# Moving the top-k of one token block out of the front of a decoder layer into its dense expert stage

## The chip, the cores and the metric

The kernel runs on one core of a Trainium2 chip. The metric is the device time of one execution in microseconds (us). The engines are named as in the profile: PE is TensorE (matmuls), DVE is VectorE, ACT is ScalarE, POOL is GpSimd, SP is SyncE (here only a queue that issues DMAs). Each engine works through its own list of instructions in order; an instruction that has to wait holds up all that stand behind it on its engine.

## What is computed

One layer of a hybrid decoder on 1024 tokens of width 1024, in float32. Its last part, where this change lies, is an expert layer (PEER) with 16384 experts of one neuron each:

```
def block(t):                                   # 128 tokens
    q = (t @ w_q).reshape(tb, 8, 2, 64)
    s = einsum('thcd,hckd->thck', q, keys)      # 8 heads, 2 halves, 128 keys
    top_s, top_i = top_k(s, 16)
    cand_s = top_s[:, :, 0, :, None] + top_s[:, :, 1, None, :]
    cand_i = top_i[:, :, 0, :, None] * 128 + top_i[:, :, 1, None, :]
    best_s, pos = top_k(cand_s, 16)
    idx = take_along_axis(cand_i, pos)          # 128 experts for each token
    g = softmax(best_s)
    act = gelu(einsum('thkd,td->thk', u_tab[idx], t))
    return einsum('thk,thkd->td', g * act, v_tab[idx])
```

Ahead of it stand a gated MLP and a state-space layer with their projections; behind it a gated residual and a final RMSNorm.

## The kernel before

The tokens are 8 blocks of 128. For blocks 0 to 4 the expert layer is computed **densely**: for each of 128 expert tiles (128 experts each) `stage1(i)` multiplies all 640 tokens by the tile's u (48 matmuls of 128x320 into `pa`, as three products of a high and a low part), applies the gelu, and `weigh` (L962) multiplies by the weights `Gt` (L968) and splits the result into `wh` and `wl` (L972). After every four tiles `stage2(g)` multiplies by their v rows (120 matmuls of 128x512 into `res` and `pd`). `load_u` and `load_v` load a tile's u and v, cast the high part on ACT (L925, L933) and subtract it on DVE (L926, L934); these are called the splits of u_i and v_i. For blocks 5, 6 and 7 the chosen rows are **gathered**: POOL issues indirect DMAs of two rows a step for each token (L878), DVE multiplies them by the token (L889, tiles `ru`), ACT sums (L884), and later DVE adds the weighted v rows (L906, tiles `rv`, one instruction a row, 128 for each block). Four row buffers of two rows each go round.

Before either, `route(b)` makes the top-k of a block: DVE's MAX8, FIND_INDEX8 and MATCH_REPLACE8 on 128 scores (L1368 to L1372), the same on the 50 candidates of a head, a softmax and look-ups of the indices (L1383 to L1430); its score tiles are `scr`, its results `gw` and `ix`. For a dense block `scatter(b)` then spreads the weights over all experts: `hot` (L675) and `a` (L680) on DVE, `b` (L688) on ACT, a matmul into `pgs` (L690), a copy to `GS` (L693) on ACT, and a store to `G_d` in DRAM, from which `load_g` reads `Gt` (L959). Block 4's scatter is the last.

The front of the program (everything up to the first dense tiles) is written out by a planner: each item of `plan` has a due time and a duration, and the items' steps are issued in the order of these. The items r0 to r7 are the routes, s0 to s4 the scatters, `ld` the first five stage 1 tiles (the lead). The scheduler of the tile framework then sets each engine's order. The main loop does one tile a turn and pulls steps of `side_work()` (L861) in between: the routes that the plan left out, three of their yields to a step, then the pool of the top-k is released, the row buffers take its place, and the gathers follow, 256 steps for each block. The two lines of the loop and of the side work that the change's numbers enter are

```
for b in range(NDB + cfg["early"], NB):          # L862, NDB = 5, NB = 8
pull(int((i + 1) * cfg["per"]) - int(i * cfg["per"]))   # L1127
```

At the end (`stage2(31)`, `finish`) DVE applies the gate, the residual and the norm (L836, L837, L845) and the rows are stored.

Of the kernel before, what the change touches and what calls it, by code (L numbers as in the profile page):

```python
# [38 lines left out]
QG = 4  # L39
GP = 2  # L40
FMAX = 3.0e38
CFG = dict(xo=[2, 3, 4, 0, 1], gt=3, ss=7, hs=2, b1=6, nw=6, raw=1, ngb=3, rows=4, lead=5, per=6.3, dv=[6, 9, 9, 2, 99], early=2,
           hp=600, eo=(2, 4), em={2: 'pppxx', 4: 'Xpp'}, seg=4, plan=dict(
    op0=(-238.2, 44.5), sb0=(-21, 248.8), m5=(-490.1, 3.4), r0=(234.1, 82.1), op1=(132.1, 27.3), op2=(292.7, 7.7),
    sb1=(310, 10.8), op3=(364.9, 36.8), r1=(301.9, 79), s0=(261.5, 137.5), sb2=(303.2, 61.7), zv=(372.6, 16.7),
    r2=(434.5, 89.3), s1=(746.9, 213.2), zu=(417.8, 124.5), sb3=(451.1, 27.3), r3=(536.2, 48.7),
    s2=(469.7, 305.5), gl=(553.5, 5.5), op4=(543.1, 6.2), op5=(577.6, 1.8), sb4=(663, 101), r4=(445.7, 88.9),
    s3=(833.5, 73.1), op6=(590.2, 7.7), sb5=(768.6, 1.7), op7=(897.9, 60.4), sb6=(809.8, 27.4), sb7=(892.4, 30.9),
    gt=(858.2, 122), rel=(739, 334), s4=(981.8, 131.5), r5=(916.4, 58.6), r6=(989.9, 124.6), ld=(776, 675.7),
    oa0=(-275.5, 62.3), oa1=(155.8, 9.5), oa2=(314.1, 7), oa3=(240.1, 5.1), oa4=(394.7, 40.1), oa5=(594, 15.7),  # L50
    oa6=(572.9, 5.5), oa7=(898.3, 28.1), z0=(-1650.9, 29.9), f1=(-1496.2, 24.1), z1=(-1253, 33.5),
    pa=(-1479.5, 58), pb=(-1364.9, 1.6), pc=(-1507.3, 44.1), cs=(-1171.2, 4.5), lu=(-1201.3, 17.4),
# [44 lines left out]
@with_exitstack  # L97
def tile_hybrid_layer(ctx: ExitStack, tc: tile.TileContext, a, out, cfg=CFG):
    nc = tc.nc
# [1383 lines left out]
```

## Time and profile before

| | us |
|---|---|
| median of 3 runs | 2657.12 (2654.34 to 2663.97) |
| the profiled execution | 2654.11 |
| its span in the profile | 2652.3 |
| PE, DVE, ACT busy | 2533.5, 2267.9, 1312.1 |
| first split of a u tile (u0) on DVE | 843.29 |
| first stage 1 tile behind the lead (pa5) on PE | 918.04 |
| last split of a u tile (u127) | 2596.07 |
| last matmul starts | 2636.74 |

Times in the trace count from the start of the span. A row of the order of time is start, duration, engine, line, operation, tiles out and in, how many alike in a row, and in brackets the idle time of the engine before it and what ended that. Buffer numbers are left out of the tiles' names there.

### The profile page before, as it was taken

How to read it: one execution, taken by the hardware profiler on the slowest of the kernel's cores; microseconds unless marked ns; L12 is line 12 of the kernel's file. 1: busy time of each engine (PE TensorE's matmuls, PEld its weight loads, DVE VectorE, ACT ScalarE, POOL GpSimd, SP SyncE). 2: the span in 40 equal slices, each digit the busy share in tenths (PEclk: the TensorE clock that was granted, in tenths of full speed). 3: DMA queues.
4: the chain of work that ended last, by engine and by line, in shares of the span. 5: the costliest groups of instructions: out<-in, count | busy, mean ns of one | idle time of the engine just before them, and what ended most of it. 6: DMA issues, size and time to landing. Idle time of an engine off the chain costs nothing.

```text
span 2652.3 us, 39046 instructions
## 1 busy us (share of the span) xinstructions
PE 2533.5 (96%) x14119; PEld 2163.7 (82%) x14119; DVE 2267.9 (86%) x4215; ACT 1312.1 (49%) x2315; POOL 1175.1 (44%) x842
## 2 busy tenths in 40 slices
PE   6999999999877999999999999999999999999997
PEld 3557676578666898889999989999999989999996
DVE  7894699869899888879989788889999888899898
ACT  2311246578968467773222577762223767732222
POOL 0001000000000177786667577766665767776660
PEclk9996999999988999999999999999999999999999
DMA  9546233444646689999999899999998999999993
GB/s 365 108 153 186 98 122 108 121 140 131 178 119 192 227 322 328 342 335 362 345 332 378 324 335 335 324 366 355 339 358 327 330 345 339 331 366 350 343 365 138
DMA packets 301761, 726.85 MB, mean 274 GB/s; under 512 B 42448, under 2 KB 133072, under 8 KB 301152
## 3 DMA queue, kind: packets, MB, share of 16 engines
q0 software_dynamic: 112832, 411.09, 42.4%
q1 hardware_dynamic: 165600, 254.48, 28.6%
q10 hardware_dynamic: 23136, 58.79, 6.2%
q8 instruction: 111, 1.82, 0.3%
q14 instruction: 82, 0.67, 0.1%
HBM read 660.70 MB, written 62.39 MB: 273 GB/s over the span
## 4 chain that ended last, share of the span: by engine, by line
PE 50%; DMA 2%; DVE 2%; issue 1%; POOL 0%; ACT 0%; DVEq 0%; POOLq 0%; ACTq 0%
PE pa L949 25%; PE res L987 13%; PE pd L996 12%; DMA ru<-in_peer_u_dram,ix 2%; DVE ru L889 1%; POOL ru L878 0%; DVE x L845 0%; DVE u L926 0%; DVE wl L972 0%; DVE x L837 0%; DVE w L968 0%; DVE v L934 0%; DVE pd L836 0%; ACT u L925 0%; ACT v L933 0%
## 5 line engine op out<-in xcount | busy, mean ns | idle before, releaser
L878 POOL DMA_INDIRECT ru<-in_peer_u_dram,ix x384 | 639.3, 1665 | 892.3 <-issue 742.3
L949 PE MATMUL pa<-Th,u 128*128 128x320 f32 x4096 | 909.5, 309 | 3.8 <-DVE u L926 2.9
L949 PEld LDWEIGHTS pa<-Th,u 128*128 128x128 f32 x4096 | 687.2, 188 | 7.0 <-DVE u L926 3.5
L878 POOL DMA_INDIRECT rv<-in_peer_v_dram,ix x384 | 515.5, 1343 | 267.8 <-DVE gacc L906 185.7
L949 PE MATMUL pa<-Tl,u 128*128 128x320 f32 x2048 | 632.7, 309 | 0.0
L889 DVE TENSOR_TENSOR ru<-ru,hn 128x2048 f32<-128x2048 f32 x192 | 438.5, 2288 | 113.7 <-DMA ru<-in_peer_u_dram,ix 111.2
L884 ACT ACTIVATE jk<-ru 128x1024 bf16<-128x1024 f32 x384 | 405.5, 1056 | 211.0 <-issue 155.3
L906 DVE SCALAR_TENSOR_TENSOR gacc<-rv,act,gacc 128x1024 f32<-128x1024 f32 x381 | 488.7, 1283 | 7.5 <-DMA rv<-in_peer_v_dram,ix 1.7
L996 PE MATMUL pd<-v,wh 128*128 128x512 f32 x1280 | 403.6, 391 | 3.4 <-ACT v L933 1.8
L987 PE MATMUL res<-v,wh 128*128 128x512 f32 x1280 | 401.1, 390 | 0.8 <-ACT wh L970 0.8
L949 PEld LDWEIGHTS pa<-Tl,u 128*128 128x128 f32 x2048 | 384.7, 188 | 1.7
L996 PEld LDWEIGHTS pd<-v,wh 128*128 128x128 f32 x1280 | 239.1, 188 | 53.2 <-ACT v L933 2.2
L987 PEld LDWEIGHTS res<-v,wh 128*128 128x128 f32 x1280 | 239.9, 188 | 50.0 <-ACT wh L970 1.1
L951 ACT ACTIVATE w<-pa 128x320 f32<-128x320 f32 x256 | 108.8, 431 | 330.8 <-PE pa L949 329.5
L688 ACT ACTIVATE b<-hot,gT 128x128 f32<-128x128 f16 x520 | 234.1, 545 | 60.7 <-PE pgs L690 35.1
L996 PE MATMUL pd<-v,wl 128*128 128x512 f32 x640 | 249.0, 390 | 1.8 <-DVE wl L972 1.8
L987 PE MATMUL res<-v,wl 128*128 128x512 f32 x640 | 248.4, 390 | 1.9 <-DVE wl L972 1.9
L690 PE MATMUL pgs<-a,b 128*128 128x128 f32 x1280 | 188.4, 299 | 48.1 <-DVE a L680 22.9
L925 ACT CAST u<-ur 128x1024 fp32r<-128x1024 f32 x128 | 133.5, 1043 | 201.5 <-DMA ur<-in_peer_ut_dram 98.1
L690 PEld LDWEIGHTS pgs<-a,b 128*128 128x128 f32 x1280 | 169.5, 206 | 70.5 <-ACT b L688 35.9
L926 DVE TENSOR_TENSOR u<-ur,u 128x1024 fp32r<-128x1024 f32 x128 | 156.4, 1222 | 30.8 <-ACT u L925 30.4
L933 ACT CAST v<-vr 128x1024 fp32r<-128x1024 f32 x128 | 133.6, 1044 | 98.9 <-DMA vr<-in_peer_v_dram 81.7
(349 smaller groups left out, 3041.0 us busy)
## 6 DMA issues: line engine op xcount, KB each, us to landing
vr<-in_peer_v_dram SPq DMA_DIRECT2D x128, 512.0 KB, 6.8
ur<-in_peer_ut_dram SPq DMA_DIRECT2D x128, 512.0 KB, 6.7
G_d<-GS SPq DMA_DIRECT2D x40, 1024.0 KB, 8.3
Gt<-G_d ACTq DMA_DIRECT2D x64, 640.0 KB, 8.0
wada<-in_w_ada_dram SPq DMA_DIRECT2D x17, 1024.0 KB, 13.7
wo<-in_w_out_dram SPq DMA_DIRECT2D x8, 1024.0 KB, 4.9
ru<-in_peer_u_dram,ix POOLq DMA_INDIRECT x384, 7.6
rv<-in_peer_v_dram,ix POOLq DMA_INDIRECT x384, 7.7
```

Source lines behind the costliest of these rows:

```text
L688: A.activation(b1[:, n], hot[:, :, o + n], AF.Copy, scale=gT[:, s1 + o + n:s1 + o + n + 1])
L690: T.matmul(pg[:, o // 4, (o % 4) * P:(o % 4 + 1) * P], b1[:, o % 2], a1[:, o % 4], start=True, stop=True)
L878: G.indirect_dma_start(out=row[:, e], out_offset=None, in_=a[src], in_offset=bass.IndirectOffsetOnAxis(ap=ix[:, s0 + e:s0 + e + 1], axis=0))
L884: A.activation(junk, row[:, e], AF.Copy, accum_out=act[:, s + e:s + e + 1])
L889: V.tensor_mul(row, row, bcast(hn, 1, GP))
L906: V.scalar_tensor_tensor(ac, row[:, e], w, ac, op0=ALU.mult, op1=ALU.add)
L925: A.copy(u[:, 0], ur)
L926: V.tensor_tensor(u[:, 1], ur, u[:, 0].bitcast(F32), op=ALU.subtract)
L933: A.copy(v[:, 0], vr)
L949: T.matmul(pa[:, :NN], l[:, k, :], r[:, k, ns], start=(k == 0 and m == 0), stop=(k == KD - 1 and m == 2))
L987: T.matmul(res[tb][n], l[:, ts], r[:, n * 512:(n + 1) * 512], start=(g == 0 and q == 0 and m == 0), stop=(g == NGR - 1 and q == QG - 1 and ...
L996: T.matmul(po, l[:, ts], r[:, n * 512:(n + 1) * 512], start=(q == 0 and m == 0), stop=(q == QG - 1 and m == 2))
```

## The change

Three numbers of the configuration. `early` goes from 2 to 1, so `side_work` does the routes of blocks 6 and 7 and not of 7 alone, 20 steps instead of 10 ahead of 768 gather steps. The item r6 leaves the plan. `per` goes from 6.3 to 6.6.

```
-... lead=5, per=6.3, dv=[6, 9, 9, 2, 99], early=2,
+... lead=5, per=6.6, dv=[6, 9, 9, 2, 99], early=1,
...
-    gt=(858.2, 122), rel=(739, 334), s4=(981.8, 131.5), r5=(916.4, 58.6), r6=(989.9, 124.6), ld=(776, 675.7),
+    gt=(858.2, 122), rel=(739, 334), s4=(981.8, 131.5), r5=(916.4, 58.6), ld=(776, 675.7),
```

What this does to the engines' orders is seen at three places. The first is DVE just ahead of the first u split, at the end of block 4's scatter (`hot4`, `a1_4`; names that end in 6 before the number are block 6's top-k). Before:

```order
L680 TENSOR_TENSOR a1_4_100_6863<-iot_1808,It4_5371 128x512
L1396 TENSOR_REDUCE sm6_6880<-g6_6877 128x8
L1416 TENSOR_TENSOR mk6_6890<-mk6_6890,dd6_6887 128x2048
L680 TENSOR_TENSOR a1_4_104_6895<-iot_1808,It4_5371 128x512
L1397 RECIPROCAL sm6_6880<-sm6_6880 128x8
L675 TENSOR_TENSOR hot4_120_6963<-iot8_1810,Jt4_5372 128x1024
L680 TENSOR_TENSOR a1_4_108_6907<-iot_1808,It4_5371 128x512
L1421 TENSOR_TENSOR mk6_6890<-mk6_6890 128x1024
L1398 TENSOR_TENSOR g6_6877<-g6_6877,sm6_6880 128x128
L680 TENSOR_TENSOR a1_4_112_6926<-iot_1808,It4_5371 128x512
L1421 TENSOR_TENSOR mk6_6890<-mk6_6890 128x512
L926 TENSOR_TENSOR u0_7023<-ur0_7021,u0_7023 128x1024
```

After:

```order
L827 TENSOR_TENSOR Tl_6567<-t32_4_6836,Th_6566 128x8x128
L675 TENSOR_TENSOR hot4_112_6764<-iot8_1810,Jt4_5372 128x1024
L680 TENSOR_TENSOR a1_4_108_6750<-iot_1808,It4_5371 128x512
L675 TENSOR_TENSOR hot4_120_6793<-iot8_1810,Jt4_5372 128x1024
L680 TENSOR_TENSOR a1_4_112_6767<-iot_1808,It4_5371 128x512
L680 TENSOR_TENSOR a1_4_116_6779<-iot_1808,It4_5371 128x512
L680 TENSOR_TENSOR a1_4_120_6796<-iot_1808,It4_5371 128x512
L926 TENSOR_TENSOR u0_6842<-ur0_6840,u0_6842 128x1024
L680 TENSOR_TENSOR a1_4_124_6808<-iot_1808,It4_5371 128x512
L1368 MAX m6_7132<-scr6_0_7134 128x8 x4
```

Block 6's instructions have left the stretch ahead of u0; its first one stands two behind u0 now.

The second is DVE in the lead, from the split of u2 to that of u3, with the two products of the weights of tiles 0 and 1 (`w0` by `Gt0_0` and `Gt0_1`). Before:

```order
L926 TENSOR_TENSOR u2_7138<-ur2_7136,u2_7138 128x1024
...
L968 TENSOR_TENSOR w0_7026<-w0_7026,Gt0_0_7309 128x2x320
L1421 TENSOR_TENSOR mk6_6890<-mk6_6890 128x1024
L1371 MAX m7_7313<-scr7_2_7337 128x8 x4
...
L926 TENSOR_TENSOR u3_7196<-ur3_7194,u3_7196 128x1024
```

After:

```order
L968 TENSOR_TENSOR w0_6845<-w0_6845,Gt0_0_7128 128x2x320
L1368 MAX m6_7132<-scr6_4_7178 128x8 x4
L1369 MAX_INDEX ixs6_7133<-m6_7132,scr6_4_7178 128x8
L926 TENSOR_TENSOR u2_6957<-ur2_6955,u2_6957 128x1024
L1369 MAX_INDEX ixs6_7133<-m6_7132,scr6_4_7178 128x8 x3
L1370 MATCH_REPLACE scr6_4_7178<-m6_7132,scr6_4_7178 128x128
L968 TENSOR_TENSOR w0_6845<-w0_6845,Gt0_1_7130 128x2x320
...
L926 TENSOR_TENSOR u3_7015<-ur3_7013,u3_7015 128x1024
```

The product with `Gt0_1` stood behind u3 before, and stands ahead of it now; the one with `Gt0_0` has moved ahead of u2.

The third is DVE from the split of u127 to that of v126 (`rv2_n` are gathered v rows n and n+1 of the last block). Before, no L906 follows u127:

```order
L906 SCALAR_TENSOR_TENSOR gacc2_19251<-rv2_126_21547,act2_16883,gacc2_19251 128x1024 x2
L926 TENSOR_TENSOR u127_21830<-ur127_21828,u127_21830 128x1024
L1025 TENSOR_TENSOR acc_6657<-acc_6657,fin2_21552 128x512
L1025 TENSOR_TENSOR acc_6657<-acc_6657,fin2_21552 128x1024 x2
L968 TENSOR_TENSOR w124_21579<-w124_21579,Gt31_1_21639 128x2x320
L836 TENSOR_TENSOR gacc2_19251<-gacc2_19251,fin2_21552 128x1024
L934 TENSOR_TENSOR v125_21841<-vr125_21839,v125_21841 128x1024
```

After:

```order
L926 TENSOR_TENSOR u127_21830<-ur127_21828,u127_21830 128x1024
L968 TENSOR_TENSOR w124_21579<-w124_21579,Gt31_0_21637 128x2x320
L906 SCALAR_TENSOR_TENSOR gacc2_18917<-rv2_114_20990,act2_16549,gacc2_18917 128x1024
L968 TENSOR_TENSOR w124_21579<-w124_21579,Gt31_1_21639 128x2x320
L906 SCALAR_TENSOR_TENSOR gacc2_18917<-rv2_114_20990,act2_16549,gacc2_18917 128x1024
L906 SCALAR_TENSOR_TENSOR gacc2_18917<-rv2_116_20995,act2_16549,gacc2_18917 128x1024
L972 TENSOR_TENSOR wl62_21837<-w124_21579,wh62_21835 128x1280
L934 TENSOR_TENSOR v125_21841<-vr125_21839,v125_21841 128x1024
L906 SCALAR_TENSOR_TENSOR gacc2_18917<-rv2_116_20995,act2_16549,gacc2_18917 128x1024
L906 SCALAR_TENSOR_TENSOR gacc2_18917<-rv2_118_21063,act2_16549,gacc2_18917 128x1024 x2
```

The last row pairs, from half of 114 to 126, stand behind u127 now, 14 instructions of L906 in all up to the split of v127.

## Rows read from the trace of the kernel before

**Rows 1.** The page: the span, and the busy time of PE and DVE.

```profile
span 2652.3 us, 39046 instructions
...
PE 2533.5 (96%) x14119; PEld 2163.7 (82%) x14119; DVE 2267.9 (86%) x4215; ACT 1312.1 (49%) x2315; POOL 1175.1 (44%) x842
```

**Rows 2.** Busy time of each engine in four stretches (columns in the first row).

```profile
core 0: us, PE busy (x) PEld busy (x) DVE busy (x) ACT busy (x) POOL busy (x), PEclk, DMA share, GB/s
...
758.20:843.30 85.10, 61.05 (x400) 55.64 (x399) 79.38 (x353) 71.97 (x159) 0.00 (x0) 0.84 0.59 174
...
901.30:905.60 4.30, 4.27 (x12) 3.37 (x13) 3.46 (x7) 1.63 (x2) 0.00 (x0) 0.61 0.40 130
...
902.00:2602.00 1700.00, 1693.52 (x9517) 1546.25 (x9516) 1475.64 (x1203) 840.50 (x1328) 1157.57 (x773) 1.00 0.93 340
2602.00:2652.00 50.00, 35.13 (x174) 30.07 (x173) 39.31 (x120) 13.16 (x30) 1.58 (x3) 0.88 0.33 116
```

**Rows 3.** What ACT waited for from 758 to 843 us.

```profile
ACT b L688 <- DVE hot L675: 6.2, 5, 2.6
ACT tq L728 <- PE pq L726: 2.7, 2, 2.1
ACT GS L693 <- PE pgs L690: 2.7, 1, 2.7
ACT Th L826 <- DMA t<-T_d: 0.8, 2, 0.5
```

**Rows 4.** DVE in order of time: u0, w0 by Gt0_1, v3, u7, u11.

```profile
843.29 1.23 DVE L926 TENSOR_TENSOR u<-ur,u 128x1024 fp32r<-128x1024 f32 x1 [0.24 <-ACT u L925]
...
871.50 0.80 DVE L968 TENSOR_TENSOR w<-w,Gt 128x640 f32<-128x640 f32 x1
...
901.31 1.22 DVE L934 TENSOR_TENSOR v<-vr,v 128x1024 fp32r<-128x1024 f32 x1 [0.88 <-ACT v L933]
...
917.28 1.23 DVE L926 TENSOR_TENSOR u<-ur,u 128x1024 fp32r<-128x1024 f32 x1 [5.02 <-ACT u L925]
...
975.27 1.22 DVE L926 TENSOR_TENSOR u<-ur,u 128x1024 fp32r<-128x1024 f32 x1
```

**Rows 5.** ACT in order of time: the last GS copies, the loads of Gt.

```profile
857.64 1.07 ACT L693 COPY GS<-pgs 128x512 f32<-128x512 f32 x2
...
865.11 1.35 ACTq L959 DMA_DIRECT2D Gt<-G_d  x2
```

**Rows 6.** PE in order of time: around 902 us, pa5, pa11.

```profile
901.33 0.50 PE L996 MATMUL pd<-v,wh 128*128 128x512 f32 x1 [1.80 <-ACT v L933]
...
903.73 0.63 PE L996 MATMUL pd<-v,wl 128*128 128x512 f32 x1
904.16 0.63 PE L987 MATMUL res<-v,wh 128*128 128x512 f32 x1
...
918.04 0.30 PE L949 MATMUL pa<-Th,u 128*128 128x320 f32 x1
...
987.35 0.46 PE L949 MATMUL pa<-Th,u 128*128 128x320 f32 x2
```

**Rows 7.** The tile Gt from 850 to 890 us: issue to landing.

```profile
DMA to landing us min/median/max: 4.0/5.6/7.5
```

**Rows 8.** DVE's groups from 918 to 2653 us: the sums of gathered v rows.

```profile
L906 DVE SCALAR_TENSOR_TENSOR gacc<-rv,act,gacc 128x1024 f32<-128x1024 f32 x381 | 488.7, 1283 | 7.5 <-DMA rv<-in_peer_v_dram,ix 1.7
```

**Rows 9.** DVE in order of time: u127, v127, the first use of res, the last product.

```profile
2596.07 1.22 DVE L926 TENSOR_TENSOR u<-ur,u 128x1024 fp32r<-128x1024 f32 x1
...
2614.43 1.22 DVE L934 TENSOR_TENSOR v<-vr,v 128x1024 fp32r<-128x1024 f32 x1
...
2623.57 0.70 DVE L836 TENSOR_TENSOR res<-res,fin 128x512 f32<-128x512 f32 x1 [5.05 <-PE res L987]
...
2647.45 1.41 DVE L845 SCALAR_TENSOR_TENSOR x<-x,rf,fin 128x512 f32<-128x512 f32 x2
```

**Rows 10.** PE in order of time: the last matmul.

```profile
2636.74 0.39 PE L996 MATMUL pd<-v,wl 128*128 128x512 f32 x1
```

More of the change, by code (lines that the diff above doesn't have):

```diff
@@ L41 @@
 FMAX = 3.0e38
-CFG = dict(xo=[2, 3, 4, 0, 1], gt=3, ss=7, hs=2, b1=6, nw=6, raw=1, ngb=3, rows=4, lead=5, per=6.3, dv=[6, 9, 9, 2, 99], early=2,
+CFG = dict(xo=[2, 3, 4, 0, 1], gt=3, ss=7, hs=2, b1=6, nw=6, raw=1, ngb=3, rows=4, lead=5, per=6.6, dv=[6, 9, 9, 2, 99], early=1,
            hp=600, eo=(2, 4), em={2: 'pppxx', 4: 'Xpp'}, seg=4, plan=dict(
```

## The prediction

> **What bounds the kernel now.** I read the page, then busy time by stretch, then the waits of the stretch that the change touches, then single engines in order of time. The page says PE: busy in 2533.5 of 2652.3 us, VectorE (DVE) in 2267.9 [rows 1]. The stretches tell more [rows 2]. Between 902 and 2602 us, the dense stage, PE is busy in 1693.5 of 1700 us: it is the bound there, and DVE has 224 us to spare. In the 85 us before the first dense tile PE is busy 61 us, DVE 79 and ACT 72: this stretch waits for DVE and ACT. In the last 50 us PE is busy 35. So the change can act on the time in three places: the front, the lead of the dense stage, and the tail; in the middle only if it makes DVE late for PE.
>
> **The front (term A).** Until 758.2 us the orders of DVE, ACT and PE are the same in both kernels. From there to u0 (843.29, [rows 4]) DVE's order loses what route(6) had there: its first-level searches in 128 scores, those in the 50 candidates, the look-ups. Counted instruction by instruction in the order and priced at the step from one start to the next, that is 29 us of the 81.6 us so counted; 52.5 stay. If DVE were the only bound, the front would be 29 us shorter. It is not: ACT's order keeps the 109 or so scatter products of L688 (one or two more fall ahead of u0, 0.9 us), the GS copies and the rest, 72.0 us busy of 85.1 [rows 2]. Its waits in 758 to 843 us [rows 3] are 6.2 us for DVE's hot (L675), 2.7 for pgs from PE, 2.7 for a projection (pq) that stays where it is, and 0.8 for T's load. The first goes, since hot now stands behind less DVE work; the second goes too, since PE was late there because DVE's a (L680) was. A = 6.2 + 2.7 - 0.9 = 8 us earlier. Bounds: 4 if half of these waits come back as others, 12 if the other waits shown go too; ACT's 72.0 us of work allow no more than 13.
>
> **The lead (term B).** Before, the split of v3 stands 58.0 us behind that of u0 (901.31 - 843.29, [rows 4]), for 54.1 us of DVE work; stage2(0) ends, and pa5 begins, 15.6 us after v3 is done (918.04, [rows 6]). After, 55.4 us of work stand ahead of v3's split. What matters more is the place of `w0 x Gt0_1` (L968): 14.9 us of work behind u0 instead of 24.5 (before, it ran at 871.50, 28.2 us behind u0, without a wait [rows 4]). Its operand comes by a chain: the last GS copy on ACT at 857.64, the store into G_d on SP, the load issued on ACT at 865.11 when that store is in [rows 5], landing 4.0 to 7.5 us later, median 5.6 [rows 7]. Relative to u0 the last GS copy moves up only from 14.4 to about 10 us, because ACT's order ahead of it hardly changes. So the load is issued at about +17, and lands at about +23, with DVE in order and waiting from +15. The cast of u2 is behind that issue on ACT, and ur2's load is behind the stores on SP: u2 comes late too, within the same wait. So 8 us of waiting, of which 3.9 (58.0 - 54.1) were there before in other places: v3 would end 65.2 us behind u0 instead of 59.2, +6.0. Six matmuls with wl1 move behind v3, since wl1 comes just ahead of it: 6 x 0.23 = 1.4 us. B = +7. Bounds: 3 with the fastest landing, 11 with the slowest and u2 behind it.
>
> **The dense stage (term C).** Route(6) and route(7) together stand in front of the first gather now. Before, the first row pair is issued at 913.28 and the first product (L889) runs after u7; after, the product stands behind u10. PE must not wait for u11, the split right behind the first five products. Before, u11 ran at 975.27 and pa11 at 987.4 [rows 4, 6]. Relative to u0, u11 had ended at 133.2; after there are 11.4 us more DVE work ahead of it (121.3 against 109.9), so 144.6; pa11 is due at 144.1 + 7 = 151. Six us stay: C = 0. From there on the order shows the same work between two u's in both kernels: 3 row pairs a tile in the u phases, 6 or 7 rows a tile in the v phases. 6.6 instead of 6.3 steps a tile does not make them denser, since the gathers run as far behind program order as the row buffers put them. Bounds: -4 and +8.
>
> **The tail (term D).** This is the largest term. Before, all 384 v rows are summed ahead of the split of u127 (2596.07). After, 370 are: 14 of L906 stand behind it, between the last splits. One takes 1.283 us [rows 8]; 14 are 18.0. DVE's work behind u127 is 47.5 us before, and 65.8 after. Before, DVE ended 52.8 us after u127's start, 5.05 of it a wait for PE's res at 2623.57 [rows 9]. After, v127's split ends 31.4 us behind u127 (19.5 before), PE has 66 matmuls behind it, 15.0 us, and ends at 46.4 (before 41.0, [rows 10]). From v127 on DVE has 34.4 us of work for PE's 15, so it never waits: it ends at 66, not 52.8. D = 18.0 - 5.05 = +13. Bounds: 9 if u127 itself comes 3 to 4 us earlier (a product w124, for which DVE waited, no longer stands ahead of it), 16 if DVE still finds 3 us to wait.
>
> **Sum.** -8 + 7 + 0 + 13 = +12 us on the profiled execution's own 2654.1 us: 2666. The median of the runs is 3.0 us above that execution, so **2669 us** for a median, 0.45% slower. A measurement of this kernel tells about 0.5% (13.3 us) from no change, so this is just inside "same".
>
> **Rivals.**
> *The front frees what DVE loses.* If ACT had room (its copies faster once DVE's port is quieter, or L688 products ahead of 758), A would come to about 20, and B would hold: 20 - 7 - 13 = 0 gain, 2657. From A over 20 it turns to a gain; with all 29, 2648. For it: DVE is busy 79 of 85 us. Against: 72 us of ACT work that no order shortens [rows 2].
>
> *Slower: the dense stage gets late at u11.* The margin is 6 us, worked out from waits of before. If the first five row pairs, all issued within the top-k's end, land late by 3 us each, u11 is 9 us late, and PE, which is the bound from there on, never gets it back: C = +9, 2678. It decides once u11 is over 6 us later than I say. For it: before, DVE waited 5.02 us for u7's cast just there [rows 4]. Against: PE lost only 6.5 us in the 1700 us of the stage before [rows 2].
>
> *Slower: the clock in the tail.* After a gap of 1.8 us at 899 to 901 us the granted clock went to 0.61 for 4.3 us, and matmuls came every 0.43 us where they came every 0.23 [rows 2, 6]: 1.2 GHz in place of 2.4. In the tail PE would wait about 5 us for v127. If the 66 matmuls behind it ran at the lower level throughout, they would take 30 us, PE would end at 61, and DVE's last 11.8 us after it (2637.1 to 2648.9, [rows 9, 10]) make 73: D = +20, 2676. If the clock is low as briefly as at 902, nothing changes, since DVE ends at 66 anyway. The Trainium skill's page "TensorE: Matmul & The Clock Gate", section "Why this matters for your kernels", warns of idle gaps between bursts of matmuls in the middle of a kernel, since the engine falls back to its lower clock; by that rule the time would be the 2676 of this rival. The rows agree on the fall and show it as short.
>
> *The change does nothing to the middle* is part of the forecast: `per` alone moves no DVE instruction that PE waits for.
>
> **How the numbers follow.** The forecast has 0.6: its own range is 2656 to 2680, and it lies on the "same" side in 0.37 and on the slower one in 0.23. The rival of the front 0.13 (faster 0.05, same 0.08), of u11 0.17 (slower 0.14), of the clock 0.10 (slower 0.09). Together: faster 0.05, same 0.49, slower 0.46. All lowest bounds together give 2653, all highest 2688; the ends of 2652 and 2684 leave out about 2 in 10.
>
> **What would show it.** Right: u0's split near 835 with ACT still busy nearly all of the 80 us before it; a DVE wait at L968 or for u2 some 15 us behind u0; pa5 at about 917, near where it was; no PE wait at u11; then the same 55 us a group; behind u127 14 L906 among the v splits, PE waiting about 5 us for v127, DVE never idle, and an end 66 us behind u127's start. Wrong: u0 before 825 (A), pa5 10 us off (B), PE waits for u11 (C), or a tail in which u127 is 10 us earlier relative to PE than before (D).

## The result and the profile after

The changed kernel takes 2673.87 us (median of 7 runs, 2671.43 to 2677.61) against 2656.73 us: 1.0063 times the kernel before, 95% interval 1.0049 to 1.0076, which is 17 us slower. The profiled execution took 2675.51 us, 21.4 more than that of before. 3.6 us of this difference lie ahead of the change, in the part of the order that both kernels share. That part ends just behind block 5's score search; its last MAX8 is the mark from which I count below. DVE in order of time before the change:

```profile
747.87 0.28 DVE L1368 MAX8 m<-scr 128x8 f32<-128x128 f32 x1
```

The page of the changed kernel, and its busy time by stretch (columns as in rows 2). The front is taken from 761.83 us on: that is the place in the order which the kernel before reaches at 758.20, 3.63 us earlier, as at the mark.

```profile
span 2673.5 us, 39095 instructions
...
PE 2547.6 (95%) x14119; PEld 2173.6 (81%) x14119; DVE 2267.4 (85%) x4215; ACT 1315.3 (49%) x2317; POOL 1171.8 (44%) x842
```

```profile
761.83:842.37 80.54, 65.25 (x412) 58.74 (x411) 52.27 (x141) 71.88 (x160) 0.00 (x0) 0.82 0.59 176
...
800.00:842.40 42.40, 30.92 (x150) 25.87 (x149) 23.93 (x34) 42.40 (x93) 0.00 (x0) 0.76 0.72 219
```

Ahead of u0, DVE is busy 52.3 us where it was 79.4 [rows 2], and yet the stretch is only 4.5 us shorter: ACT has the same work (72.0 us before, 71.9 now), and is busy in 42.40 of the last 42.40 us. Its longest wait from 761.83 us on (the others add up to 0.7 us):

```profile
ACT tq L728 <- PE pq L726: 8.0, 2, 5.2
```

The waits for hot (6.2 in [rows 3]) and for pgs (2.7) are gone but for 0.2 us; the one for the projection pq grew from 2.7 to 8.0. PE in order of time shows why: in either kernel it works through 112 matmuls of pq in one piece. Before, and then after:

```profile
768.86 12.67 PE L726 MATMUL pq<-tq,wq 128*128 128x128 f32 x112
```

```profile
773.94 12.67 PE L726 MATMUL pq<-tq,wq 128*128 128x128 f32 x112
```

They end 33.7 us behind the mark before and 35.1 after. What ACT saves ahead of that place it spends there, waiting for pq. From there to u0 it is 61.8 us before and 55.8 after: these 6.0 us, less the 1.4 by which pq came later, are all that the front gains.

DVE in order of time: the mark, u0, u1, a wait for block 6's scores, u2, w0 by Gt0_1, v3, u11.

```profile
751.50 0.28 DVE L1368 MAX8 m<-scr 128x8 f32<-128x128 f32 x1
...
842.37 1.23 DVE L926 TENSOR_TENSOR u<-ur,u 128x1024 fp32r<-128x1024 f32 x1 [0.52 <-ACT u L925]
...
851.06 1.21 DVE L926 TENSOR_TENSOR u<-ur,u 128x1024 fp32r<-128x1024 f32 x1
...
867.54 0.87 DVE L1368 MAX8 m<-scr 128x8 f32<-128x128 f32 x4 [7.71 <-DMA scr<-sc_d]
868.60 1.21 DVE L926 TENSOR_TENSOR u<-ur,u 128x1024 fp32r<-128x1024 f32 x1
870.77 0.81 DVE L968 TENSOR_TENSOR w<-w,Gt 128x640 f32<-128x640 f32 x1
...
911.12 1.21 DVE L934 TENSOR_TENSOR v<-vr,v 128x1024 fp32r<-128x1024 f32 x1
...
985.32 1.22 DVE L926 TENSOR_TENSOR u<-ur,u 128x1024 fp32r<-128x1024 f32 x1
```

DVE stood still for 7.7 us, not at Gt0_1 but for scores, and u2's split began 17.5 us after u1's. SP's queue shows what lay ahead of both loads, and ACT's order when ur2 was in:

```profile
851.62 2.16 SPq L696 DMA_DIRECT2D G_d<-GS  x2
853.87 3.61 SPq L923 DMA_DIRECT2D ur<-in_peer_ut_dram  x1
857.58 1.91 SPq L762 DMA_DIRECT2D scr<-sc_d  x2
```

```profile
856.88 1.61 ACTq L959 DMA_DIRECT2D Gt<-G_d  x2
...
865.92 1.04 ACT L925 CAST u<-ur 128x1024 fp32r<-128x1024 f32 x1 [6.95 <-DMA ur<-in_peer_ut_dram]
```

The two last stores, 1 MB each, then ur2, then the scores. ur2's load came 12 us after its issue began, and the DMA engines were busy all that time (share 1.01; columns as in rows 2):

```profile
853.80:866.00 12.20, 5.40 (x37) 5.14 (x36) 4.05 (x24) 0.52 (x2) 0.00 (x0) 0.89 1.01 316
```

The longest of PE's waits from 843 to 927 us, for u2's cast, follows from it:

```profile
PE pa L949 <- ACT u L925: 7.8, 1, 7.8
```

PE in order of time: pa5, pa11, pa125, the last matmuls.

```profile
926.52 0.30 PE L949 MATMUL pa<-Th,u 128*128 128x320 f32 x1
...
995.83 0.46 PE L949 MATMUL pa<-Th,u 128*128 128x320 f32 x2
...
2601.54 0.30 PE L949 MATMUL pa<-Th,u 128*128 128x320 f32 x1
...
2656.90 0.39 PE L996 MATMUL pd<-v,wl 128*128 128x512 f32 x1
2657.13 0.62 PE L996 MATMUL pd<-v,wh 128*128 128x512 f32 x2
2657.58 0.39 PE L996 MATMUL pd<-v,wl 128*128 128x512 f32 x1
```

PE's longest wait in the tail:

```profile
PE pd L996 <- DVE x L837: 3.9, 1, 3.9
```

PE in order of time behind this wait, and the granted clock there (0.68, the column behind POOL's): from 2651.9 to 2654.9 us a matmul comes every 0.43 us, where it is 0.23 at the end of the tail.

```profile
2650.63 0.73 PE L996 MATMUL pd<-v,wh 128*128 128x512 f32 x2 [3.88 <-DVE x L837]
...
2653.21 0.63 PE L996 MATMUL pd<-v,wl 128*128 128x512 f32 x1
2653.64 1.05 PE L996 MATMUL pd<-v,wh 128*128 128x512 f32 x2
```

```profile
2650.00:2655.00 5.00, 4.37 (x13) 3.44 (x14) 4.93 (x24) 2.02 (x6) 0.00 (x0) 0.68 0.00 0
```

The tail on DVE: u127, v127, the first wait behind them, the last product; the wait of 5.05 us for res [rows 9] is gone.

```profile
2606.47 1.22 DVE L926 TENSOR_TENSOR u<-ur,u 128x1024 fp32r<-128x1024 f32 x1
...
2637.02 1.22 DVE L934 TENSOR_TENSOR v<-vr,v 128x1024 fp32r<-128x1024 f32 x1
...
2644.97 1.30 DVE L836 TENSOR_TENSOR res<-res,fin 128x512 f32<-128x512 f32 x2 [0.19 <-PE res L987]
...
2668.73 1.42 DVE L845 SCALAR_TENSOR_TENSOR x<-x,rf,fin 128x512 f32<-128x512 f32 x2
```

**The time by stage.** Five marks cut an execution: the MAX8 above, the start of u0's split, pa5, pa125 (the first stage 1 tile behind the second-last stage 2; 2588.62 before, the row below), and the end of DVE's last instruction.

```profile
2588.62 0.30 PE L949 MATMUL pa<-Th,u 128*128 128x320 f32 x1
```

So before: 843.29 - 747.87 = 95.4 us, 74.7, 1670.6 and 60.2. The same subtractions for every profiled execution (names as in the experiments below):

| | front | lead | dense stage | tail |
|---|---|---|---|---|
| before | 95.4 | 74.7 | 1670.6 | 60.2 |
| before, 14 rows cut | 95.0 | 74.3 | 1673.1 | 59.9 |
| before, b shared | 101.0 | 75.0 | 1672.5 | 59.9 |
| after | 90.9 | 84.1 | 1675.0 | 68.6 |
| after, pace 6.3 | 90.7 | 84.3 | 1675.4 | 68.6 |
| after, 14 rows cut | 91.9 | 84.1 | 1680.3 | 60.3 |
| after, stores by POOL | 91.5 | 80.5 | 1672.0 | 71.5 |
| after, ur by POOL | 91.9 | 81.2 | 1671.0 | 68.6 |
| after, b shared | 87.3 | 77.9 | 1672.8 | 67.9 |
| after, b shared, stores by POOL | 87.4 | 76.4 | 1670.4 | 69.0 |
| after, b shared, ur by POOL | 87.4 | 78.6 | 1672.5 | 67.9 |
| after, tail on POOL | 91.5 | 86.1 | 1682.5 | 74.0 |
| after, all three | 87.2 | 76.3 | 1668.7 | 74.1 |

Front, lead and tail repeat within about 2 us where the order is the same; the dense stage varies by several. The stretch ahead of the first mark (747 to 756 us) varies too. So the single stages say more than the totals.

### The profile page after: what moved, and what is told of

It reads as the page before. It is cut to its first block, busy times and chain, and to the rows that moved or that the text cites. A ratio compares the mean times of both kernels' runs of the same rounds, so it can differ in the third digit from the quotient of the medians.

```text
span 2673.5 us, 39095 instructions
## 1 busy us (share of the span) xinstructions
PE 2547.6 (95%) x14119; PEld 2173.6 (81%) x14119; DVE 2267.4 (85%) x4215; ACT 1315.3 (49%) x2317; POOL 1171.8 (44%) x842
## 5 line engine op out<-in xcount | busy, mean ns | idle before, releaser
L878 POOL DMA_INDIRECT ru<-in_peer_u_dram,ix x384 | 626.6, 1632 | 946.4 <-PE pd L996 706.0
L878 POOL DMA_INDIRECT rv<-in_peer_v_dram,ix x384 | 524.8, 1367 | 256.2 <-DVE gacc L906 167.3
L906 DVE SCALAR_TENSOR_TENSOR gacc<-rv,act,gacc 128x1024 f32<-128x1024 f32 x381 | 489.1, 1284 | 7.4 <-DMA rv<-in_peer_v_dram,ix 1.3
L690 PE MATMUL pgs<-a,b 128*128 128x128 f32 x1280 | 191.5, 302 | 35.1 <-DVE a L680 11.9
```

The costliest lines, as they stand in the source:

```text
L690: T.matmul(pg[:, o // 4, (o % 4) * P:(o % 4 + 1) * P], b1[:, o % 2], a1[:, o % 4], start=True, stop=True)
L878: G.indirect_dma_start(out=row[:, e], out_offset=None, in_=a[src], in_offset=bass.IndirectOffsetOnAxis(ap=ix[:, s0 + e:s0 + e + 1], axis=0))
L906: V.scalar_tensor_tensor(ac, row[:, e], w, ac, op0=ALU.mult, op1=ALU.add)
```

## The experiments

Each ratio is to runs of the kernel before that were taken together with the experiment.

**Only the pace put back.** Block 6's route stays in the dense stage.

```
-    per=6.6, ... early=1
+    per=6.3, ... early=1
```

> Block 6's top-k in the dense stage, but 6.3 steps a tile instead of 6.6. Theory: the pace number moves nothing that matters, the order of DVE has the same 14 row sums behind u127; the time is that of the changed kernel, 17 us over the kernel before (13 to 21). Rival, the pace costs it: the time falls at least half way back, to 8 us over the kernel before or less.

Measured: 1.0077 (1.0048 to 1.0105), and every stage as in the changed kernel within 0.4 us. The pace number costs nothing and gives nothing here; the loss comes from where the route stands.

**The 14 row sums behind u127 taken away**, in either kernel. The last block's sum lacks its last 14 expert rows.

```
-            for s in range(0, NS, GP):
+            for s in range(0, NS - 14 if n == NGB - 1 else NS, GP):
                 row = fetch("peer_v", s, "rv")
```

> The changed kernel without the last 14 of the 128 gathered v rows of the last block: seven row fetches and 14 row sums fewer, so the 14 that stood behind u127 are gone. Theory: they are what DVE ends late with; 14 x 1.28 = 18 us of DVE work go, DVE waits for PE again as before, and the time falls by 8 to 13 us against the changed kernel, to 4 to 9 us over the kernel before. Rival, the end is set by PE's last matmuls and the norm behind them: it falls by less than 4 us.

> The kernel before without the last 14 of the 128 gathered v rows of the last block. There the row sums end ahead of u127 and DVE waits 5 us for PE at the end. Theory: the same 14 rows are worth 0 to 3 us here. Rival, row sums cost DVE's time wherever they stand, because DVE is the bound of the last stage: 8 us or more faster than the kernel before.

Measured: 1.0043 (1.0025 to 1.0061) for the changed kernel, 1.0003 (0.9989 to 1.0017) for the one before. The tail went from 68.6 to 60.3 us, to what it is in the kernel before (60.2), and there the same 14 rows were worth 0.3. In the medians the gain is 5 us, less than the 8 to 13 expected. In the profiled execution the dense stage was 5 us longer, which hides part of the tail's gain; of the other executions no stage is known, and the two intervals leave room for 8 us. DVE in order of time shows the wait for PE back:

```profile
2638.02 0.70 DVE L836 TENSOR_TENSOR res<-res,fin 128x512 f32<-128x512 f32 x1 [4.11 <-PE res L987]
```

So the tail's loss is these 14 row sums, and a row sum costs nothing while it stands ahead of the last splits.

**The last two stores from another queue.**

```
-                nc.sync.dma_start(G_d[...], GS[i]...)
+                (nc.gpsimd if b == 4 and q == 3 else nc.sync).dma_start(G_d[...], GS[i]...)
```

> The changed kernel with the last two stores of the weights (the fourth quarter of block 4's scatter into G_d) issued from POOL's queue instead of SP's, so that the loads of ur2 and of block 6's scores don't stand behind them. The scheduler then puts w0 by Gt0_1 at 22 us of DVE work behind u0 instead of 15. Theory, the lead loses its 9 us to loads that are late behind the two stores on SP: pa5 stands 76 to 80 us behind u0 instead of 84, and the time falls by 4 to 8 us. Rival, the loads are late because the stores fill the DMA engines, whichever queue issues them: pa5 stays 82 us or more behind u0, and the time falls by less than 3 us.

Measured: 1.0040 (1.0022 to 1.0057). The lead is 80.5 us, 3.6 shorter: just outside what the theory asked for, and less than the rival allowed. SP and ACT in order of time:

```profile
854.96 0.33 SPq L923 DMA_DIRECT2D ur<-in_peer_ut_dram  x1
```

```profile
861.38 1.05 ACT L925 CAST u<-ur 128x1024 fp32r<-128x1024 f32 x1 [6.96 <-DMA ur<-in_peer_ut_dram]
```

ur2 now took 6.4 us from issue to cast instead of 12. The queue was about half of its delay; the rest was not taken apart. The tail grew to 71.5 in this order: u127's split stands 12.4 us behind pa125 instead of 4.9, and PE waited 2.3 us for v127 instead of 0.7.

**The loads of ur1 to ur4 from POOL's queue**, with the stores left on SP.

```
-        nc.sync.dma_start(ur, a["peer_ut"][i])
+        (nc.gpsimd if 0 < i < 5 else nc.sync).dma_start(ur, a["peer_ut"][i])
```

> The changed kernel with the loads of ur1 to ur4 issued from POOL's queue instead of SP's; the last stores and the loads of block 6's and 7's scores stay on SP, the scores' loads now ahead of the last stores. Theory, the lead is lost to ur2 behind the two last stores: ur2's load takes 4 to 6 us from the split of u1 instead of 13, pa5 stands 74 to 79 us behind u0 instead of 84. Rival, the stores fill the DMA engines whichever queue the load is on: pa5 82 us or more behind u0.

Measured: 1.0042 (1.0028 to 1.0056), lead 81.2 us: between the two again. POOL, ACT and DVE in order of time say why:

```profile
858.31 0.54 POOL L923 DMA_DIRECT2D ur<-in_peer_ut_dram  x1 [8.49 <-DVE ixs L1369]
```

```profile
863.26 1.55 ACTq L959 DMA_DIRECT2D Gt<-G_d  x2
864.86 0.77 ACT L951 ACTIVATE w<-pa 128x320 f32<-128x320 f32 x2 [7.10 <-PE pa L949]
865.50 1.05 ACT L925 CAST u<-ur 128x1024 fp32r<-128x1024 f32 x1
```

```profile
869.83 0.83 DVE L968 TENSOR_TENSOR w<-w,Gt 128x640 f32<-128x640 f32 x1 [1.02 <-DMA Gt<-G_d]
```

The cast of u2 no longer waits for its load but stands behind the issue of Gt on ACT (its wait is put down to PE's pa; PE had nothing from u2 to work on), and DVE waits for Gt0_1. That is the chain on which the prediction built term B. It is there, a little shorter than the one through SP, which hid it: the lead is only 2.9 us shorter.

**A third of the b products on DVE**, in either kernel.

```
-    dv=[6, 9, 9, 2, 99]
+    dv=[6, 9, 9, 2, 3]
```

> The changed kernel, with every third pair of block 4's b products (22 of 64) made by DVE (0.61 us each pair) instead of by ACT (two of 0.43 us each). Theory, without block 6's top-k the front waits for ACT: ACT loses 19 us of work ahead of u0, DVE has 28 us to spare and gets 13; u0 comes 6 to 14 us earlier, measured from 758 us, and the time falls by 5 to 12 us against the changed kernel. Rival, the front waits for the projections on PE or for loads: u0 moves by less than 3 us.

> The same share of b products on DVE in the kernel before. There DVE is busy 79 of the 85 us ahead of u0. Theory, DVE and ACT are both nearly full there: DVE's work ahead of u0 grows by 9 us, u0 comes 2 to 9 us later, and the time rises by 2 to 9 us. Rival, ACT bounds the front of the kernel before too: the time falls by 4 us or more.

Measured: 1.0016 (1.0007 to 1.0026) for the changed kernel, so 10 to 12 us gained; 1.0030 (1.0020 to 1.0040) for the one before, 8 us lost. The front went from 90.9 to 87.3 us in the one and from 95.4 to 101.0 in the other. Busy time up to u0, first after and then before, both with b shared:

```profile
754.00:838.00 84.00, 66.77 (x458) 59.49 (x458) 71.14 (x198) 66.69 (x142) 0.00 (x0) 0.91 0.64 192
```

```profile
753.00:851.00 98.00, 71.06 (x428) 65.04 (x427) 94.88 (x401) 64.05 (x134) 0.00 (x0) 0.75 0.55 163
```

Before, DVE is busy 94.9 of 98 us: it bounds that front. Take the route away and it no longer does. The front gained less than the 6 us expected, since ACT still waits 9.1 us for pq: from the end of pq's matmuls to u0 it is 49.9 us where it was 55.8, but pq ended 2.3 us later. The lead gained 6.2 as well, which I had not expected: in this order the two last stores and ur2 no longer meet. SP in order of time, the stores, and behind ur1 and two loads of scores ur2 and ur3:

```profile
834.07 3.48 SPq L696 DMA_DIRECT2D G_d<-GS  x2
...
851.08 9.33 SPq L923 DMA_DIRECT2D ur<-in_peer_ut_dram  x2
```

**The last acc products on POOL.**

```
-                V.tensor_mul(ap, ap, fin[0][:, sl])
-                V.tensor_add(xs[tb][:, sl], xs[tb][:, sl], ap)
+                G.tensor_mul(ap, ap, fin[0][:, sl])
+                G.tensor_add(xs[tb][:, sl], xs[tb][:, sl], ap)
```

> The changed kernel, with the six last products and sums of acc (L1025, L1026), 5.9 us of DVE work behind u127, made by POOL, which is idle then. Theory, DVE is the bound behind u127: the end comes 3 to 6 us earlier, measured from pa125. Rival, the end waits for PE's last matmuls or POOL's results: less than 2 us, or later.

Measured: 1.0088 (1.0071 to 1.0105), the tail 74.0 us, 5.4 longer instead of 3 to 6 shorter. POOL and DVE in order of time:

```profile
2642.18 8.58 POOL L1025 TENSOR_TENSOR acc<-acc,fin 128x512 f32<-128x512 f32 x3 [2.08 <-DMA fin<-gt_d]
```

```profile
2641.69 10.15 DVE L906 SCALAR_TENSOR_TENSOR gacc<-rv,act,gacc 128x1024 f32<-128x1024 f32 x4
...
2654.28 1.22 DVE L934 TENSOR_TENSOR v<-vr,v 128x1024 fp32r<-128x1024 f32 x1
```

Four row sums, 4 x 1.283 us [rows 8] elsewhere, took 10.15 while POOL multiplied. One of POOL's three products, and the row sum beside it:

```profile
2644.08 3.37 POOL L1025 TENSOR_TENSOR acc<-acc,fin 128x1024 f32<-128x1024 f32 x1
```

```profile
2645.24 3.30 DVE L906 SCALAR_TENSOR_TENSOR gacc<-rv,act,gacc 128x1024 f32<-128x1024 f32 x1
```

The order also put v127's split behind the last block's residual, and PE waited 6.1 us for it. That the end moved with what slows DVE fits a tail whose path runs through DVE, but the order changed as well; the edit did not relieve DVE.

**All three, and pairs of them.**

> The changed kernel with all three: shared b products, the last two stores of G_d on POOL's queue, the last acc products on POOL. If each takes away its own loss: 6 to 14 us from the front, 3 to 4 from the lead, 3 to 6 from the tail, together 12 to 22 us, which is 0 to 5 us under the kernel before. If they get in each other's way (the stores at the same time as more DVE work): 5 us or more above the kernel before.

> The changed kernel with every third pair of block 4's b products on DVE and the last two stores of G_d on POOL's queue, without the acc products on POOL. Front 87 us from the last block 5 score search to u0 (91 in the changed kernel, 95 before), lead 76 to 77 (84; 75), tail 68 (69; 60). The sum is 2 us under to 4 us over the kernel before, so this should be 0.999 to 1.002 of it. If the lead's and the front's gains don't hold in other executions: 1.004 or more.

> The changed kernel with every third pair of block 4's b products on DVE and the loads of ur1 to ur4 on POOL's queue. If both act on their own part: front 87 us, lead 72 to 77, tail 66 to 69, 0.997 to 1.001 of the kernel before. If ur1 to ur4 are not what the lead waits for once b is shared: the same as with the shared b products alone, 1.0016.

Measured: all three 1.0018 (1.0006 to 1.0031), 4.5 us over the kernel before and so between the two expectations, the tail on POOL eating what the others gave; b shared with the stores on POOL 0.9992 (0.9980 to 1.0004), 2657.92 us; b shared with ur on POOL 1.0007 (0.9995 to 1.0018). The total of this last one is as expected, but its lead of 78.6 us is no shorter than with b shared alone (77.9), so there the lead does not wait for ur1 to ur4. The second undoes the loss, with a front 8.0 us under that of before, the lead at 76.4 and the tail still at 69.0. It does not beat the kernel before beyond the interval.

## Why the prediction was off by 5 us, step by step

The forecast was +12 us, the stages of the two profiled executions give -4.5 + 9.4 + 4.4 + 8.4 = +17.7 behind the mark, the medians +17.1. The signs were right for the front, the lead and the tail; the sizes were not, and in the lead the wait stood elsewhere. The errors of the four terms, +3.5, +2.4, +4.4 and -4.6, cancel in part, so that a total off by 5 us is partly luck.

**Term A**, -8 predicted, -4.5 measured. The two waits went as predicted (hot from 6.2 us to none, pgs from 2.7 to 0.2), and ACT's own work stayed the same (72.0 and 71.9). What failed is the step at pq, "that stays where it is". The projection did stay, at 33.7 and 35.1 us behind the mark, and just because of that the wait for it grew by 5.3 us: ACT, which works in order, came to it earlier. So the waits saved ahead of pq were no gain; only those behind it were. That ACT takes over as the bound behind pq was right, and the two runs with b shared show it: the same edit helps the one kernel and hurts the other.

**Term B**, +7 predicted, +9.4 measured. Its main chain was the wrong one. I let DVE wait at w0 by Gt0_1, with u2 "late too, within the same wait"; in fact DVE never waited there, and u2's load and block 6's scores were late behind the two last stores. The time reckoned for Gt0_1 was near, though. In the run with only the pace put back, which has the changed kernel's order, its load is the longer of the two loads of Gt issued between 850 and 890 us. It landed 25.1 us behind u0, where I had said 23:

```profile
DMA to landing us min/median/max: 7.9/8.9/10.0
```

In the changed kernel u2's cast began 23.6 us and the search in block 6's scores 25.2 us behind u0. So three late loads arrive within about 2 us of each other, and that the term came near its size is partly luck. It also fits that two runs which each took one part away gained only 3.6 and 2.9 us; the second then showed the Gt0_1 chain itself. What is left over the kernel before (6 us) was not taken apart further. A slip in the sum changes little: 55.4 us of work and 8 of waiting are 5.4 more than 58.0, and not 6.0.

**Term C**, 0 predicted, +4.4 measured, inside its bounds of -4 and +8. The step at u11 held: it was done at 986.5, pa11 began at 996.0, so the margin was 9 us and not 6, and the rival that would have made the dense stage late there is out. PE's busy time from pa5 to pa125, before and then after (columns as in rows 2):

```profile
918.04:2588.62 1670.58, 1664.10 (x9361) 1519.82 (x9360) 1453.99 (x1175) 829.90 (x1315) 1152.66 (x768) 1.00 0.93 343
```

```profile
926.52:2601.54 1675.02, 1666.97 (x9362) 1520.68 (x9361) 1458.38 (x1263) 833.67 (x1319) 1137.41 (x759) 1.00 0.93 338
```

So 1.6 of the 4.4 us are idle time of PE, and 2.9 are matmuls that took longer. PE's waits are short ones, mostly for wh and wl up to 1300 us, and behind one of them the clock was low: a wait for wh ended at 1001.6, and from 1003.6 to 1010 us the granted clock was 0.76.

The table says more about this term than one execution does. The four executions with the changed kernel's order up to the tail (after, pace 6.3, 14 rows cut, tail on POOL) took 1675.0 to 1682.5 us in the dense stage. The three of the kernel before and its variants took 1670.6 to 1673.1, and the six whose lead was reordered 1668.7 to 1672.8. So this order costs some 2 to 12 us here, and part of what the other orders gained in total lies in this stage. Which place in the order brings the waits was not taken apart.

**Term D**, +13 predicted, +8.4 measured, just under its bound of 9. The mechanism is shown by the 14 rows cut in both kernels. Two things made it smaller: DVE ended 63.7 us behind u127 and not 66, and u127 itself came 2.5 us earlier relative to PE (4.9 us behind pa125 and not 7.4), as the bound had allowed. PE ended at 51.5 us behind u127, not 46.4, since it waited 3.9 us for DVE's residual (L837) ahead of pd, and the 14 matmuls behind this wait took 4.9 us instead of 3.2; DVE still had the last word.

**The clock in the tail** did fall, but behind another wait than the rival's, and briefly. PE waited only 0.7 us for v127. Behind its 3.9 us wait for the residual the granted clock was 0.68 from 2650 to 2655 us, and matmuls came every 0.43 us, the lower level of 1.2 GHz; from 2655.5 us on they came every 0.23 again. DVE waited 0.2 us for PE in the whole tail, so nothing of this reached the end. The Trainium skill's page "TensorE: Matmul & The Clock Gate", section "Why this matters for your kernels", warns of idle gaps between bursts of matmuls in the middle of a kernel. The trace agrees on the fall behind the 3.9 us wait, and shows it as short.

**The front that frees it all** is out: 27.1 us less of DVE's busy time made 4.5 us. ACT's copies and products did not get faster beside a quieter DVE either: ACT's work stayed at 71.9 us.

## What to carry to other kernels

Work that leaves a busy engine gives only what the next engine has to spare: read the second-busiest engine's time in that stretch, and look for the places where it will wait for a third (here pq). Then change what it does as well: sharing its products made the front 3.6 us shorter here, and 5.6 us longer where DVE was still full. A step that is moved takes its loads along: look in the queue's order for what they now stand next to, above all large stores ahead of a load with a single buffer. Work that trails a pipelined stage is free until it reaches the last tiles; count how many of its instructions stand behind the last one that the bound engine needs.

## What the hardware showed that I had not expected

While POOL multiplied 128x2560 values (8.58 us for what DVE does in 2.95, L1025 in the tail before), four of DVE's row sums took 10.15 us in place of 5.1. The last two took 3.30 and 3.27 us, and each ended 1.1 us after one of POOL's products, as if it did its work only when POOL was done; the reason was not tested. In the run with all three edits POOL's product took 8.46. A load of 512 KB issued behind two stores of 1 MB on the same queue took 12 us to arrive, and 6.4 when the stores were issued from another queue at nearly the same time.
